# A two-layer decoder trunk on one core: weight sums of twelve pairs a layer built in DRAM by accumulating transfers, and the last down block as seven products

## Chip, core and metric

The kernel runs on one core of a Trainium2 chip. The metric is the device time of one execution in microseconds. The kernel before was timed three times: 1818.12, 1818.70 and 1818.74 us, with a median of 1818.7 us. A separate execution was profiled; all durations of single instructions come from it.

The engines are named as in the profile: PE multiplies matrices (PEld is its load of stationary operands), DVE, ACT and POOL work elementwise, SP issues most DMAs. POOL can issue DMAs as well, and only its DMAs can accumulate into their destination.

## The reference

The trunk has two layers on 512 tokens of width 1024, in float32. The part that matters here is the feed-forward half of a layer, with W1 of 1024 x 4096 and W2 of 4096 x 1024:

```python
def hybrid_layer(x, ...):
    ...
    x = x + rmsnorm(mix, post_mix_g)

    h2 = rmsnorm(x, pre_mlp_g)
    ff = jnp.square(jax.nn.relu(h2 @ w_ff1)) @ w_ff2
    return x + rmsnorm(ff, post_mlp_g)
```

Ahead of it in each layer come one wide projection, a gated delta rule, a banded attention with sinks, two up-projections and an output projection (`mix`). The change leaves their matrix products as they are.

## The kernel before

**Products.** Each float32 operand is split in two fp32r parts, a rounded one (`wh`, `P_h`) and the rest (`wl`, `P_l`), and each product is three matmuls: high x high, high x low, low x high. The split of a weight block `wr` of 128 x 1024 costs a cast on ACT (L384) and a subtraction on DVE (L385). `weights()` hands the blocks out in the order of `chunk_order` and prepares them four ahead (`LOOK = 4`, four buffers each of `wh` and `wl`); `wr` has six buffers, filled by DMAs that SP issues.

**Feed-forward.** The 4096 hidden units go in four blocks `s` of 1024, each as eight units `m` of 128. A block is first computed ("up", `ff1`) and then multiplied with its 1024 rows of W2 ("down"); `acc[t][n]` holds the sum over the blocks for token tile `t` (128 tokens) and column half `n`. A single unit is 24 matmuls of 512 columns (L400 to L402). A pair of units, written as a tuple in `SEQ`, is computed by seven products of half size instead of eight: 84 matmuls of 256 columns (L487 to L490). It needs two sums of the weight blocks, which DVE makes with four additions of 128 x 512 (L343). Before the change `SEQ` holds no pair in block 0, two in block 1, three in block 2 and four in block 3, nine in a layer.

**Down.** Blocks 0 to 2 take seven products too: P1 to P7, each 24 matmuls of 512 columns (`mm_c`, L475 to L479), with left factors from the hidden units (`lefts`, `make`) and right factors that are sums of W2 blocks (`seven`, additions at L304 and L309). The seven run in the order P1, P5, P6, P2, P7, P3, P4; P6 continues on a negated copy of P1's result (`py`), and P7 on a copy of P6's (`pw_`). Block 3 is an ordinary product: `mm_b4` for the first column half of all four token tiles (96 matmuls) and `last_tiles`, or a plain loop in the last layer, for the second half (96 matmuls), one token tile after the other, so that each tile's norm runs beside the next tile's matmuls.

**Norms.** `ff2_tail` calls `post_tiles`: a sum of squares on ACT (`meansq`, L520), a multiplication by the gain (L575), a power on POOL (`rstd`, L526), two multiply-adds with the residual (L578, L579) and, if another layer follows, the same once more for the next norm (L525, L535), ending in `xs`, which PE transposes (`norm_turn`, L546).

**Order.** Instructions are recorded in program order and a scheduler lays them out, one list for each engine; an engine runs its list in that order. `Order` pins some engines to program order for a stretch, and `tc.keep_in_program_order` does so for one instruction.

Of the kernel before, what the change touches and what calls it, by code (L numbers as in the profile page):

```python
# [15 lines left out]
ALU = mybir.AluOpType  # L16
# [28 lines left out]
SEQ = (FF_ORDER, (0, 1, (4, 5), (2, 3), 6, 7), ((0, 1), (4, 5), (2, 3), 6, 7), ((0, 1), (2, 3), (4, 5), (6, 7)))  # L45
# [12 lines left out]
def chunk_order(depth):  # L58
# [3 lines left out]
    for l in range(depth):  # L62
# [65 lines left out]
def hybrid_trunk(ctx, tc, x, positions, pre_mix_g, dn_conv_w, dn_a_log, dn_dt_bias, dn_norm_g,  # L128
# [162 lines left out]
    def seven(w, l, r0):  # L291
# [15 lines left out]
        def both(j):  # L307
# [10 lines left out]
                 lambda j: add(1, 0, j))  # L318
        return [(lambda f=f, j=j: f(j), 512) for f in makes for j in range(2)]


    def up_specs(l, s):
# [7 lines left out]
        def one(ms):  # L330
            b = {}

            def raw():
                b["0"], b["1"] = (unit(m) for m in ms)
                return b["0"]

            def of(n_):
                b[n_] = wp.tile([P, 1024], F32, name="wr", bufs=WR)
                x0, x1, x2, x3 = b["0"][:, :512], b["0"][:, 512:], b["1"][:, :512], b["1"][:, 512:]
                yb = b["a"][:, 512:]  # L340
                for o_, i0, i1 in (((b[n_][:, :512], x0, x2), (yb, b[n_][:, :512], x3)) if n_ == "a" else
                                   ((b[n_][:, 512:], x2, x3), (b[n_][:, :512], yb, x1))):
                    tt(out=o_, in0=i0, in1=i1, op=ALU.add)  # L343
                return b[n_]

            return raw, lambda: of("a"), lambda: of("b"), lambda: b["1"][:, 512:]
# [13 lines left out]
        return out + [(last, -1)] * bool(last)  # L360

# [104 lines left out]
    def mm_c(pss, left, onto=False, js=range(2)):  # L466

        for j in js:
            wh, wl = weights()
            hi, lo = left[j]  # L470
            for t in range(2):
# [87 lines left out]
    def post_tiles(tiles, a0g, ps1, q0, gb, xsrc, xdst, gb2=None, Tx=(T[5], T[6], T[7])):  # L559


        n = range(len(tiles))
        rows = [slice(t * P, (t + 1) * P) for t in tiles]
# [10 lines left out]
        for i, t in enumerate(tiles):  # L574
            tt(out=xo[i][:, 512:], in0=a[i], in1=gb[:, 512:], op=ALU.mult)  # L575
            r.append(rstd("pr", q0[t], q1[i]))
        for i, t in enumerate(tiles):
            stt(out=xo[i][:, :512], in0=a0g[t], scalar=r[i], in1=xt[i][0], op0=ALU.mult, op1=ALU.add)  # L578
            stt(out=xo[i][:, 512:], in0=xo[i][:, 512:], scalar=r[i], in1=xt[i][1], op0=ALU.mult,  # L579
                op1=ALU.add)  # L580
            xdst(t, xo[i])
# [23 lines left out]
    for l in range(depth):  # L605
# [437 lines left out]
        late, klate = (), []  # L1043
        for i in range(16):
            us = []
# [249 lines left out]
        for m in range(KT):  # L1295
# [5 lines left out]
            steps(2 if m < 6 else 40)  # L1301
            if m == 1:
                turn0()
# [66 lines left out]
        mm_b4(pss, mT)  # L1370
        m0, s0 = [], []
# [51 lines left out]
        def ff2_tail(tiles, pss):  # L1423
            a0 = [a[0] for a in acc]
            Tx = T[0], T[3], T[6]
            if l == depth - 1:
                post_tiles(tiles, a0, pss, s0, gb3, xd, give, None, Tx)
            else:
                xs_next.extend(post_tiles(tiles, a0, pss, s0, gb3, xd, keep, nxt[0], Tx))
# [35 lines left out]
        def ff1(done, rest=None):  # L1465
# [4 lines left out]
            for n, e in enumerate(SEQ[s]):  # L1470
                if not isinstance(e, tuple):
# [35 lines left out]
                mm_h(y, c2, 4, ops["n2"], False)  # L1507
# [5 lines left out]
                mm_h(z, c2, 0, ops["n1"], False)  # L1513
# [18 lines left out]
        for s in range(3):  # L1532
# [9 lines left out]
            def lefts(X, Y):  # L1542

                a11, a21, a12, a22 = X[:, 0:512], X[:, 512:1024], Y[:, 0:512], Y[:, 512:1024]
                make("P1", T[5], a11)
# [5 lines left out]
                make("P4", T[2], a22, -1.0)  # L1551
# [142 lines left out]
```

## Time and profile before

| what | value |
|---|---|
| median of three runs | 1818.7 us |
| profiled execution, device time | 1816.19 us |
| its span | 1814.5 us |
| granted TensorE clock, mean | 0.999 |
| ACT busy | 1007.5 us (56%) |
| POOL busy | 210.6 us (12%) |
| DMA | 278.60 MB, mean 154 GB/s |
| first layer, from the first down product to the next layer's first matmul | 625.8 to 909.7 us |

The profiled execution is 2.5 us, or 0.14%, under the median; 1.7 us of its time lie outside the span. In the profile, a timeline row gives the start, the duration, the engine and line, and in brackets how long the engine had stood idle and what ended that. Matmuls overlap, so their pace is read from the distance of their starts and not from the duration of one.

### The profile page before, as it was taken

Reading aid. Unit: us, or ns where it says so; the run is one execution under the profiler, and the core shown is the slowest. Engines: PE = TensorE matmul, PEld = TensorE weight load, DVE = VectorE, ACT = ScalarE, POOL = GpSimd, SP = SyncE. Lnnn points to the kernel's source line nnn. Section 1 sums busy time; section 2 is a strip of 40 time slices with the busy share of each in tenths; the row PEclk is TensorE's granted clock in tenths of the full one; section 3 lists DMA queues with packets and bytes.
Section 4 is the critical chain, followed back from the end, with each engine's and each line's share of the span. In section 5 each row is a group of like instructions: output and inputs, shape, how many; then the busy total and the mean of one; then the engine's idle time right before and its main releaser. Section 6 shows DMA issues by size and latency. Waiting matters only on the chain.

```text
span 1814.5 us, 28394 instructions
## 1 busy us (share of the span) xinstructions
PE 1794.6 (99%) x10252; PEld 1524.7 (84%) x10252; DVE 1375.1 (76%) x2590; ACT 1007.5 (56%) x2065; POOL 210.6 (12%) x386
## 2 busy tenths in 40 slices
PE   9999999999999999999999999999999999999998
PEld 8878878888788888989898887888877888889896
DVE  5499796887666878898556997968875669698973
ACT  6678742444434656566556877234443347566572
POOL 0322102221101000000013221022111010000000
PEclk9999999999999999999999999999999999999999
DMA  5633447655463254554445334585545533555551
GB/s 201 203 112 121 111 146 226 178 172 152 117 208 129 82 164 156 174 180 145 168 160 176 106 127 111 169 232 159 163 140 154 171 116 105 174 162 164 174 178 56
DMA packets 146431, 278.60 MB, mean 154 GB/s; under 512 B 33569, under 2 KB 66657, under 8 KB 146290
## 3 DMA queue, kind: packets, MB, share of 16 engines
q1 hardware_dynamic: 145778, 276.75, 49.2%
q8 instruction: 81, 1.33, 0.3%
q14 instruction: 60, 0.49, 0.1%
q0 software_dynamic: 512, 0.03, 0.0%
HBM read 239.38 MB, written 37.36 MB: 153 GB/s over the span
## 4 chain that ended last, share of the span: by engine, by line
PE 88%; DVE 4%; ACT 4%; DMA 2%; issue 1%; POOL 0%; SPq 0%; DVEq 0%; POOLq 0%; ACTq 0%
PE ps_b L459 3%; PE ps_b L461 3%; PE ps_b L463 3%; PE ps_f L400 2%; PE ps_f L401 2%; PE ps_f L402 2%; PE ps_us L400 2%; PE ps_ud L400 2%; PE ps_us L401 2%; PE ps_ud L401 2%; PE ps_ud L402 2%; PE ps_us L402 2%; PE ps_vp L400 2%; PE ps_vp L402 2%; PE ps_vp L401 1%; PE ps_qp L401 1%
## 5 line engine op out<-in xcount | busy, mean ns | idle before, releaser
L384 ACT CAST wh<-wr 128x1024 fp32r<-128x1024 f32 (+2 forms) x368 | 372.7, 1019 | 430.4 <-PE ps_us L401 60.2
L385 DVE TENSOR_TENSOR wl<-wr,wh 128x1024 fp32r<-128x1024 f32 (+2 forms) x368 | 434.9, 1189 | 183.8 <-ACT wh L384 180.2
L526 POOL TENSOR_TENSOR pr<-pq,pw 128x1 f32<-128x1 f32 x16 | 9.8, 615 | 790.1 <-DVE pq L525 790.1
L459 PE MATMUL ps_b<-wh,h_h 128*128 128x432 f32 (+1 forms) x192 | 71.1, 370 | 0.0
L461 PE MATMUL ps_b<-wl,h_h 128*128 128x432 f32 (+1 forms) x192 | 70.4, 367 | 0.0
L463 PE MATMUL ps_b<-wh,h_l 128*128 128x432 f32 (+1 forms) x192 | 70.3, 366 | 0.0
L400 PE MATMUL ps_f<-g_h,wh 128*128 128x512 f32 x160 | 62.4, 390 | 0.0
L401 PE MATMUL ps_f<-g_l,wh 128*128 128x512 f32 x160 | 62.4, 390 | 0.0
L402 PE MATMUL ps_f<-g_h,wl 128*128 128x512 f32 x160 | 62.2, 389 | 0.0
L401 PE MATMUL ps_qp<-h_l,wh 128*128 128x512 f32 x128 | 53.9, 421 | 0.0
L400 PE MATMUL ps_vp<-h_h,wh 128*128 128x512 f32 x128 | 53.7, 420 | 0.0
L402 PE MATMUL ps_vp<-h_h,wl 128*128 128x512 f32 x128 | 53.7, 419 | 0.0
L995 ACT ACTIVATE M<-M,nm 128x128 f32<-128x128 f32 x128 | 49.8, 391 | 5.9 <-DVE nm L990 5.8
L400 PE MATMUL ps_qp<-h_h,wh 128*128 128x512 f32 x128 | 51.8, 405 | 0.0
L343 DVE TENSOR_TENSOR wr<-wr 128x512 f32<-128x512 f32 x72 | 47.5, 685 | 5.5 <-DMA wr<-in_weights_dram 5.2
L400 PE MATMUL ps_kp<-h_h,wh 128*128 128x512 f32 x128 | 51.6, 403 | 0.0
L402 PE MATMUL ps_qp<-h_h,wl 128*128 128x512 f32 x128 | 51.4, 401 | 0.0
L401 PE MATMUL ps_vp<-h_l,wh 128*128 128x512 f32 x128 | 51.3, 401 | 0.0
L401 PE MATMUL ps_ga<-h_l,wh 128*128 128x512 f32 x128 | 51.0, 398 | 0.0
L400 PE MATMUL ps_gb<-h_h,wh 128*128 128x512 f32 x128 | 51.0, 398 | 0.0
L402 PE MATMUL ps_kp<-h_h,wl 128*128 128x512 f32 x128 | 50.9, 398 | 0.0
L402 PE MATMUL ps_ga<-h_h,wl 128*128 128x512 f32 x128 | 50.7, 396 | 0.0
(435 smaller groups left out, 5928.4 us busy)
## 6 DMA issues: line engine op xcount, KB each, us to landing
wr<-in_weights_dram SPq DMA_DIRECT2D x320, 512.0 KB, 3.6
wr<-in_weights_dram SPq DMA_DIRECT2D x24, 432.0 KB, 5.2
D<-dd SPq DMA_DIRECT2D x32, 256.0 KB, 2.7
xd<-xo SPq DMA_DIRECT2D x12, 512.0 KB, 3.0
xt<-xd SPq DMA_DIRECT2D x24, 256.0 KB, 4.5
D<-gd SPq DMA_DIRECT2D x16, 256.0 KB, 6.2
dd<-D SPq DMA_DIRECT2D x16, 256.0 KB, 5.2
kkd<-kk SPq DMA_DIRECT2D x16, 256.0 KB, 2.0
```

The source lines that it names most:

```text
L343: tt(out=o_, in0=i0, in1=i1, op=ALU.add)
L384: nc.scalar.copy(wh[:, :w], wr[:, :w])
L385: sub(out=wl[:, :w], in0=wr[:, :w], in1=wh[:, :w].bitcast(F32), op=ALU.subtract)
L400: mm(ps, lhsT=wh[:, k, :], rhs=hi, start=k == 0, stop=False)
L401: mm(ps, lhsT=wh[:, k, :], rhs=lo, start=False, stop=False)
L402: mm(ps, lhsT=wl[:, k, :], rhs=hi, start=False, stop=k == KT - 1)
L459: mm(pss[t], lhsT=hi[:, tsl], rhs=wh[:, r, :], start=k == 0 and not onto, stop=False, skip_group_check=onto)
L461: mm(pss[t], lhsT=hi[:, tsl], rhs=wl[:, r, :], start=False, stop=False, skip_group_check=onto)
L463: mm(pss[t], lhsT=lo[:, tsl], rhs=wh[:, r, :], start=False, stop=k == KT - 1, skip_group_check=onto)
L526: ptt(out=r, in0=q1, in1=mhalf[:, 0:1], op=ALU.pow)
L995: act(out=M[:, j * P:(j + 1) * P], in_=M[:, j * P:(j + 1) * P], func=AF.Exp, bias=nm[:, j:j + 1], accum_out=den[:, j:j + 1])
```

## The change

**Pairs.** Blocks 1, 2 and 3 now run as four pairs each, twelve in a layer. The weight sums of a pair are made in DRAM scratch: `prepare` copies the two units' blocks there with two SP DMAs of 512 KB, then POOL issues three accumulating DMAs of 512, 256 and 256 KB. Each of the fifteen calls of `next(ready)` in a layer starts one pair and moves up to three others on by one stage. `one` then loads the finished sums, two whole blocks and a half, in the place of DVE's additions.

**Down block 3.** It runs as seven products like the others, in the order P1, P5, P6, P2, P3, P7, P4. Before P2 and P3, DVE adds the accumulated `acc` of token tiles 0 and 1 onto the partial results in PSUM (`pa`, `pv`). After P3, tiles 0 and 1 are complete and `ff2_tail` runs for both; after P7, DVE puts `acc` of tiles 2 and 3 onto `pw_`, and P4 completes them. In the last layer P4 runs for tile 2 first and then for tile 3. P1's left factor is made earlier, and in the order of PSUM pools `pa` and `py` change places in blocks 1 to 3.

```diff
-SEQ = (FF_ORDER, (0, 1, (4, 5), (2, 3), 6, 7), ((0, 1), (4, 5), (2, 3), 6, 7), ((0, 1), (2, 3), (4, 5), (6, 7)))
+FF_PAIRS = ((0, 1), (4, 5), (2, 3), (6, 7))
+SEQ = (FF_ORDER, FF_PAIRS, FF_PAIRS, FF_PAIRS)
...
             out.append(("up", l, s))
-            if s < 3:
-                out.append(("seven", "w_ff2", l, s * 1024))
-                continue
-            for n in range(2):
-                for j in range(4):
-                    b_in("w_ff2", s * 1024 + j * 256, n * 512, 512)
+            out.append(("seven", "w_ff2", l, s * 1024))
...
+        if r0 == 3072:
+            makes = makes[:4] + (makes[5], makes[4], makes[6])
...
         def one(ms):
-            b = {}
-
-            def raw():
-                b["0"], b["1"] = (unit(m) for m in ms)
-                return b["0"]
-
-            def of(n_):
-                b[n_] = wp.tile([P, 1024], F32, name="wr", bufs=WR)
-                x0, x1, x2, x3 = b["0"][:, :512], b["0"][:, 512:], b["1"][:, :512], b["1"][:, 512:]
-                yb = b["a"][:, 512:]
-                for o_, i0, i1 in (((b[n_][:, :512], x0, x2), (yb, b[n_][:, :512], x3)) if n_ == "a" else
-                                   ((b[n_][:, 512:], x2, x3), (b[n_][:, :512], yb, x1))):
-                    tt(out=o_, in0=i0, in1=i1, op=ALU.add)
-                return b[n_]
-
-            return raw, lambda: of("a"), lambda: of("b"), lambda: b["1"][:, 512:]
+            d = sums[l, s, ms]
+
+            def of(c, w=1024):
+                wr = wp.tile([P, 1024], F32, name="wr", bufs=WR)
+                dma(wr[:, :w], d[:, c * 1024:c * 1024 + w])
+                return wr
+
+            def tail():
+                wr = wp.tile([P, 1024], F32, name="wr", bufs=WR)
+                dma(wr[:, :512], wpk[index["w_ff1", l, 0, (s * 8 + ms[1]) * P, 0], :, 512:])
+                return wr
+
+            return lambda: unit(ms[0]), lambda: of(0), lambda: of(1), tail
...
+    pairs = [(s_, e) for s_, seq in enumerate(SEQ) for e in seq if isinstance(e, tuple)]
+    sums = {(l, *p): dr.tile([P, 2048], F32, name=f"fs{l}{p[0]}{p[1][0]}")
+            for l in range(depth) for p in pairs}
+    def prepare(l):
+        here = tc.keep_in_program_order
+        def stages(s_, e):
+            i = index["w_ff1", l, 0, (s_ * 8 + e[0]) * P, 0]
+            assert index["w_ff1", l, 0, (s_ * 8 + e[1]) * P, 0] == i + 1
+            v = sums[l, s_, e][:, :].rearrange("p (h t c) -> p h t c", h=2, t=2)
+            for t in range(2):
+                here(dma(v[:, :, t, :], wpk[i + t].rearrange("p (h c) -> p h c", h=2)))
+            yield
+            here(pdma(v[:, :, 1, :], wpk[i:i + 2, :, 0:512].rearrange("t p c -> p t c"),
+                      accum_op=ALU.add))
+            yield
+            here(pdma(v[:, 0, 0, :], v[:, 1, 1, :], accum_op=ALU.add))
+            yield
+            here(pdma(v[:, 1, 0, :], v[:, 0, 0, :], accum_op=ALU.add))
+        todo = [stages(*p) for p in pairs]
+        for n in range(len(todo) + 3):
+            for g in todo[max(n - 3, 0):n + 1]:
+                next(g, None)
+            yield
...
+        ready = prepare(l)
         for i in range(16):
+            if i in (0, 2, 4, 6, 8, 11, 14):
+                next(ready)
...
-        for s in range(3):
+        for s in range(4):
...
+                if ms[-1] in (1, 3):
+                    make("P1", T[5], raw[0][:, 0:512])
...
             make_later("P3", T[1])
+            if s == 3:
+                break
...
-        ff1(done, pending)
-        pss = [b("ps_b4") for b in (PZ, PS, PS, PZ)]
-        for t in range(NT):
-            nc.scalar.copy(pss[t], acc[t][0])
-        mm_b4(pss, h3, onto=True)
-        for t in range(NT):
-            s0[t] = meansq(pss[t], "pq0")
-            tt(out=acc[t][0], in0=pss[t], in1=gb3[:, :512], op=ALU.mult)
-        ws = [weights() for _ in range(4)]
+        def early_half(t, n, src):
+            s0[t] = meansq(src, "pq0")
+            tt(out=acc[t][n], in0=src, in1=gb3[:, n * 512:(n + 1) * 512], op=ALU.mult)
+        for t in range(2):
+            tt(out=pa[t], in0=pa[t], in1=acc[t][0], op=ALU.add)
+            tt(out=pv[t], in0=pv[t], in1=acc[t][1], op=ALU.add)
         if l < depth - 1:
             nxt = pre_begin(l + 1)
             xs_next = []
+        mm_c(pa, left["P2"], True)
+        for t in range(2):
+            early_half(t, 0, pa[t])
+        mm_c(pv, left["P3"], True)
+        ff2_tail((0, 1), pv)
+        mm_c(pw_, left["P7"], True)
+        for t in range(2):
+            tt(out=acc[2 + t][1], in0=pw_[t], in1=acc[2 + t][1], op=ALU.add)
+            tt(out=pw_[t], in0=acc[2 + t][0], in1=pw_[t], op=ALU.subtract)
+        for t in range(2):
+            early_half(2 + t, 1, acc[2 + t][1])
+        if l < depth - 1:
             order = Order(nc.tensor)
             order.begin()
-            last_tiles(ws, h3, "ps_f2", ff2_tail, lambda t: norm_turn(xs_next[t], t, nxt[1]),
-                       [a[1] for a in acc])
+            for j in range(2):
+                mm_c(pw_, left["P4"], True, (j,))
+                norm_turn(xs_next[j], j, nxt[1])
+            ff2_tail((2, 3), pw_)
             hT = nxt
         else:
-            for t in range(NT):
-                ps = (PS if t % 2 else PZ)("ps_f2")
-                nc.scalar.copy(ps, acc[t][1])
-                mm_b(ps, ws, h3, t, onto=True)
-                ff2_tail((t,), [ps])
+            ws = [weights() for j in range(2)]
+            for t in range(2):
+                mm_c(pw_, left["P4"], True, ts_=(t,), ws=ws)
+                ff2_tail((2 + t,), pw_[t:])
```

**How the rows move.** The first place is DVE's list in the first layer's block 3. The names end in the program's buffer numbers: `ps_b4` are the four results of `mm_b4`, `h3_l` a split hidden unit, `ps_py`, `ps_pa` and `ps_pv` the partial results of P6, P1/P2 and P5/P3. Before, ahead of the first tile's norm:

```order
L501 TENSOR_TENSOR h3_l_9220<-raw_9051,h3_h_9219 128x512
L385 TENSOR_TENSOR wl_9264<-wr_9261,wh_9263 128x1024
L385 TENSOR_TENSOR wl_9294<-wr_9291,wh_9293 128x1024
L385 TENSOR_TENSOR wl_9324<-wr_9321,wh_9323 128x1024
L1653 TENSOR_TENSOR acc_6596<-ps_b4_9223,gb_8672 128x512
L1653 TENSOR_TENSOR acc_6598<-ps_b4_9224,gb_8672 128x512
```

And now, from P6 to P2:

```order
L409 TENSOR_TENSOR wl_9593<-wr_9590,wh_9592 128x1024
L1448 TENSOR_TENSOR acc_6665<-ps_py_9508,acc_6665 128x512
L1448 TENSOR_TENSOR acc_6667<-ps_py_9509,acc_6667 128x512
L525 TENSOR_TENSOR P3_l_9613<-S2_9206,P3_h_9612 128x512
L1683 TENSOR_TENSOR ps_pa_9468<-ps_pa_9468,acc_6664 128x512
L525 TENSOR_TENSOR P3_l_9617<-S2_9451,P3_h_9616 128x512
L1684 TENSOR_TENSOR ps_pv_9520<-ps_pv_9520,acc_6665 128x512
L1683 TENSOR_TENSOR ps_pa_9469<-ps_pa_9469,acc_6666 128x512
```

The additions onto `ps_pa` stand behind the two that read P6's result `ps_py`. On PE, the same place now reads:

```order
L503 MATMUL ps_py_9509<-wh_9525,P6_l_9459 128x512
L499 MATMUL ps_pa_9468<-wh_9543,P2_h_9512 128x512
L501 MATMUL ps_pa_9468<-wl_9544,P2_h_9512 128x512
L503 MATMUL ps_pa_9468<-wh_9543,P2_l_9513 128x512
L499 MATMUL ps_pa_9468<-wh_9543,P2_h_9512 128x512
L501 MATMUL ps_pa_9468<-wl_9544,P2_h_9512 128x512
L503 MATMUL ps_pa_9468<-wh_9543,P2_l_9513 128x512
L499 MATMUL ps_pa_9469<-wh_9543,P2_h_9512 128x512
```

P2, which writes `ps_pa`, follows P6 directly there; six matmuls go onto `ps_pa_9468` before the first onto `ps_pa_9469`.

The second place is DVE's list at the end of the first layer, around the norms of tiles 0 and 1. Before, where `xo` and `xs` belong to one tile at a time:

```order
L575 TENSOR_TENSOR xo_9430<-ps_f2_9397,gb_8672 128x512
L525 SCALAR_TENSOR_TENSOR pq1_9432<-pq1_9432,pq0_9352 128x1
L578 SCALAR_TENSOR_TENSOR xo_9430<-acc_6596,pr_9435,xt_9426 128x512
L579 SCALAR_TENSOR_TENSOR xo_9430<-xo_9430,pr_9435,xt_9427 128x512
L525 SCALAR_TENSOR_TENSOR nq1_9445<-nq1_9445,nq0_9442 128x1
L535 SCALAR_TENSOR_TENSOR xs_9450<-xo_9430,nr_9447,gb_9391 128x512
L535 SCALAR_TENSOR_TENSOR xs_9452<-xo_9430,nr_9447,gb_9391 128x512
L575 TENSOR_TENSOR xo_9483<-ps_f2_9398,gb_8672 128x512
```

And now, from the last multiply-add of tile 1 on, where `ps_pw` is the result of P7 that P4 goes on with:

```order
L604 SCALAR_TENSOR_TENSOR xo_9728<-xo_9728,pr_9740,xt_9722 128x512
L549 SCALAR_TENSOR_TENSOR nq1_9753<-nq1_9753,nq0_9750 128x1
L409 TENSOR_TENSOR wl_9779<-wr_9382,wh_9778 128x1024
L559 SCALAR_TENSOR_TENSOR xs_9764<-xo_9727,nr_9761,gb_9626 128x512
L559 SCALAR_TENSOR_TENSOR xs_9766<-xo_9727,nr_9761,gb_9626 128x512
L549 SCALAR_TENSOR_TENSOR nq1_9759<-nq1_9759,nq0_9756 128x1
L409 TENSOR_TENSOR wl_9797<-wr_9794,wh_9796 128x864
L559 SCALAR_TENSOR_TENSOR xs_9771<-xo_9728,nr_9768,gb_9626 128x512
L559 SCALAR_TENSOR_TENSOR xs_9773<-xo_9728,nr_9768,gb_9626 128x512
L1695 TENSOR_TENSOR acc_6669<-ps_pw_9569,acc_6669 128x512
L1696 TENSOR_TENSOR ps_pw_9569<-acc_6668,ps_pw_9569 128x512
```

The two additions on `ps_pw_9569`, which P4 waits for, stand behind the whole norm chain of both tiles. In the second layer no next norm follows, and between the last multiply-add and the additions stands one `wl` row alone.

The third place is POOL's list beside the attention of the first layer, where `pc` is a masked probability tile that PE multiplies next, `irk` a power of the key norms, and `fs` a pair's scratch. Now:

```order
L1042 AFFINE_SELECT pc_1515<-pf_l_1510 128x512
L378 DMA fs010_112<-fs010_112 128x512
L376 DMA fs014_113<-fs014_113 128x512
L373 DMA fs012_114<-in_weights_dram 256x1x512
L854 TENSOR_TENSOR irk_1576<-ssk_1570,pw_93 128x4
L1042 AFFINE_SELECT pc_1652<-pf_h_1648 128x512
```

Before, the same rows stand there without the three DMAs.

More of the change, by code (lines that the diff above doesn't have):

```diff
@@ L1370, in hybrid_trunk @@
         mm_b4(pss, mT)
+        next(ready)
         m0, s0 = [], []
@@ L1584, in hybrid_trunk @@
                     done((m,), ps)
+                    if s == 0 and i in (1, 5):
+                        next(ready)
                     if s == 0 and i in (1, 3, 5):
```

46 lines of the change are left out of this document (23 added, 23 removed).

## The prediction

> **What bounds the kernel now.** I read the page's busy shares first, then PE's own list of waits, then the pace of its matmuls, and last who works beside it in a down block.
>
> ```profile
> span 1814.5 us, 28394 instructions
> PE 1794.6 (99%) x10252; PEld 1524.7 (84%) x10252; DVE 1375.1 (76%) x2590; ACT 1007.5 (56%) x2065; POOL 210.6 (12%) x386
> PE 88%; DVE 4%; ACT 4%; DMA 2%; issue 1%; POOL 0%; SPq 0%; DVEq 0%; POOLq 0%; ACTq 0%
> ```
>
> PE is busy for 99% of the span and holds 88% of the chain that ended last. So the time is the number of matmuls at their pace, plus whatever makes PE wait. Its longest waits of before, from the view of waits on PE alone:
>
> ```profile
> PE ps_pt L1007 <- ACT M L1001: 3.9, 6, 0.8
> PE ps_row L602 <- DMA row<-in_pre_mix_g_dram: 2.3, 1, 2.3
> ```
>
> The first lies in the attention, the second at the start; no line of the feed-forward is worth a microsecond. The pace comes from the timeline of PE: the first and last of 97 matmuls of 256 columns in a row, and of 24 of 512 columns.
>
> ```profile
> 759.83 0.28 PE L490 MATMUL ps_q<-n_h,wl 128*128 128x256 f32 x1
> ...
> 771.35 0.28 PE L490 MATMUL ps_z<-n_h,wl 128*128 128x256 f32 x1
> ```
>
> ```profile
> 606.57 0.39 PE L402 MATMUL ps_f<-g_h,wl 128*128 128x512 f32 x1
> ...
> 611.78 0.39 PE L401 MATMUL ps_f<-g_l,wh 128*128 128x512 f32 x1
> ```
>
> The distance of starts is 11.52/96 = 0.120 us for 256 columns and 5.21/23 = 0.2265 us for 512. The 0.28 and 0.39 us in the rows overlap and would be wrong as a price: by them a pair would cost more than two single units.
>
> Who has room beside PE? One down block of before and the up block behind it, DVE alone:
>
> ```profile
> 785.63:826.00 40.37, 38.88 (x47) 1.00 0.49 156
> ```
>
> DVE is busy for 38.88 of 40.37 us. In a down block PE is the bound by a hair, and DVE, which makes weight splits, weight sums and left factors, is the engine that any new dependency meets.
>
> **The change part by part.**
>
> **Matmuls.** Three pairs a layer replace six single units: 6 x 24 = 144 matmuls of 512 columns go and 3 x 84 = 252 of 256 come. The last down block goes from 192 to 168, and one filler matmul (L1603) is added. Over two layers that is 2 x (-144 - 24 + 1) = -334 matmuls of 512 and +504 of 256: -334 x 0.2265 + 504 x 0.120 = -75.7 + 60.5 = **-15.2 us**. A pair saves only 10.88 - 10.08 = 0.8 us, the down block 5.4.
>
> **DVE's pair sums.** They go:
>
> ```profile
> L343 DVE TENSOR_TENSOR wr<-wr 128x512 f32<-128x512 f32 x72 | 47.5, 685 | 5.5 <-DMA wr<-in_weights_dram 5.2
> ```
>
> The 47.5 us lie beside PE's matmuls in up blocks, where PE does not wait, so I count them at nothing.
>
> **From P6 to P2, twice.** Here a wait is added: P2 must find `acc` already added onto `pa`. P6 and its neighbours already run in the blocks before, so their rows price it. DVE, ACT and PE there (the PE rows are the first of the block, that is of P1, and the first after P6; the last fence has DVE's first row of the block):
>
> ```profile
> 796.82 2.36 DVE L385 TENSOR_TENSOR wl<-wr,wh 128x1024 fp32r<-128x1024 f32 x2
> 799.10 0.68 DVE L1417 TENSOR_TENSOR acc<-ps_pv,acc 128x512 f32<-128x512 f32 x1
> ...
> 802.57 1.28 DVE L1417 TENSOR_TENSOR acc<-ps_py,acc 128x512 f32<-128x512 f32 x2
> 803.77 0.68 DVE L501 TENSOR_TENSOR P_l<-S,P_h 128x512 fp32r<-128x512 f32 x1
> ```
>
> ```profile
> 801.03 0.57 ACT L1606 COPY ps_pw<-ps_py 128x512 f32<-128x512 f32 x1 [0.96 <-PE ps_py L479]
> 802.39 0.57 ACT L1606 COPY ps_pw<-ps_py 128x512 f32<-128x512 f32 x1 [0.79 <-PE ps_py L479]
> ```
>
> ```profile
> 785.63 0.39 PE L475 MATMUL ps_pa<-wh,P_h 128*128 128x512 f32 x1
> ...
> 802.19 0.39 PE L475 MATMUL ps_pa<-wh,P_h 128*128 128x512 f32 x1
> ```
>
> ```profile
> 787.85 0.69 DVE L1547 TENSOR_TENSOR S<-raw 128x512 f32<-128x512 f32 x1
> ```
>
> DVE paces a 128 x 512 row at 0.60 us (802.57 to 803.77 holds two) and a 128 x 1024 row at 1.14 (796.82 to 799.10 holds two). P6's halves can be read 1.16 us before and 0.20 us after its end. In the order of the change, DVE has 13 short and 7 long rows between the first `S` and the first `acc<-ps_py`: 13 x 0.60 + 7 x 1.14 = 15.8 us. `S` starts 2.2 us after P1 (787.85, with P1 at 785.63), and P6 ends 3 x 5.44 + 0.23 = 16.55 us after P1's start, so that `acc<-ps_py` starts 1.45 us after the end of P6. Then come two `acc`, one `P3_l` and the first `ps_pa`: 4 x 0.60, and P2 starts at 3.85. Three short rows more, and the second `ps_pa` is ready at 5.65, where P2 wanted it at 1.36. PE loses 4.3 us a layer, **+8.6 us**. Bounds: with an idle DVE the rows can begin at 0.20 and the loss is 2.45 us; with the weight splits late by 0.7 us it is 5.0.
>
> **From P7 to P4, twice.** Count from the moment the second `ps_pa` is ready. PE ends P3 9.5 us later (P2 and P3 are 48 matmuls, less the first six: 42 x 0.2265) and P7 at 15.0. DVE first has 3 short and 8 long rows, 10.9 us, and stands about 1.15 us behind a weight sum whose cast ACT must make first. The norms of tiles 0 and 1 start at 12.05, 2.5 us after the end of P3. Rows of the same chain at the layer's end before:
>
> ```profile
> 910.72 0.69 DVE L575 TENSOR_TENSOR xo<-ps_f,gb 128x512 f32<-128x512 f32 x1 [0.55 <-ACT jk L520]
> 911.33 0.15 DVE L525 SCALAR_TENSOR_TENSOR pq<-pq,pq 128x1 f32<-128x1 f32 x1
> ...
> 912.06 0.75 DVE L579 SCALAR_TENSOR_TENSOR xo<-xo,pr,xt 128x512 f32<-128x512 f32 x1
> 912.72 0.75 DVE L578 SCALAR_TENSOR_TENSOR xo<-acc,pr,xt 128x512 f32<-128x512 f32 x1
> 913.38 0.75 DVE L579 SCALAR_TENSOR_TENSOR xo<-xo,pr,xt 128x512 f32<-128x512 f32 x1
> 914.04 0.15 DVE L525 SCALAR_TENSOR_TENSOR nq<-nq,nq 128x1 f32<-128x1 f32 x1
> 914.11 1.05 DVE L385 TENSOR_TENSOR wl<-wr,wh 128x864 fp32r<-128x864 f32 x1
> ...
> 917.81 1.42 DVE L535 SCALAR_TENSOR_TENSOR xs<-xo,nr,gb 128x512 f32<-128x512 f32 x2 [0.72 <-POOL nr L526]
> ```
>
> Two `xo` and two sums take 1.45 us and four multiply-adds at 0.66 take 2.65; with what POOL leaves open they end 6.8 us after P3. In the second layer one split (1.14) and two additions (1.2) follow: P4 may start at 9.15, P7 ended at 5.44, a loss of 3.7 us. In the first layer the split, two times two `xs` (1.33 each), a split of 864 columns (1.0) and POOL's round trips stand ahead of the additions, which end at 13.05: 7.6 us. Together **+11.3 us**. Bounds: had DVE no backlog, the norms would start 2.95 us sooner, with 1.2 and 5.0 us lost, POOL's turns taking some of it back; another microsecond late makes 4.7 and 8.6. Queued behind the additions are the splits for the next layer's first block, which are not needed for another 5 us.
>
> **The clock.** After its last matmul, starting at 1807.04, PE stands idle:
>
> ```profile
> 1807.50:1810.50 3.00, 0.00 (x0) 0.00 (x0) 1.51 (x4) 0.69 (x2) 0.54 (x1) 1.00 0.00 0
> 1811.00:1814.50 3.50, 0.00 (x0) 0.00 (x0) 0.16 (x1) 0.00 (x0) 0.00 (x0) 0.50 0.40 150
> ```
>
> The 1.00 and the 0.50, third from the end of a row, are the granted clock: it falls to half within 3.7 us. The first layer's idle of 7.6 us is longer than that, so P4 begins at half clock. If its first twelve matmuls ran so, they would cost 2.7 us more; at nothing if the clock came back at once. No row tells; I take the middle, **+1.4 us**. The Trainium skill, "TensorE: Matmul & The Clock Gate", part 1, has a clock that halves after about 3.4 us of idleness and returns after about 3.4 us of work; the trace agrees with the fall, and by that figure the cost would be some 1.7 us, an estimate by that page.
>
> **The end.** P4 gives tile 3 only 12 matmuls after tile 2, and the norm of tile 2 still holds DVE.
>
> ```profile
> 1808.27 0.69 DVE L575 TENSOR_TENSOR xo<-ps_f,gb 128x512 f32<-128x512 f32 x1 [2.55 <-ACT jk L520]
> ```
>
> Before, tile 3's `xo` started about 1.0 us after PE's end; now 1.3: **+0.3 us**, between 0 and 0.6.
>
> **Transfers.** Twelve pairs add 25 MB of copies and accumulations a layer, and pairs and down block load some 14 MB more: 78 MB on 278.60 in all. They lie beside PE; a weight block is asked for four blocks ahead, and a load takes 3.6 us:
>
> ```profile
> wr<-in_weights_dram SPq DMA_DIRECT2D x320, 512.0 KB, 3.6
> ```
>
> Four blocks are 10.9 us in a down block. I count nothing. Without that cover, one late load would cost its delay.
>
> **The sum** is -15.2 + 8.6 + 11.3 + 1.4 + 0.3 = +6.4 us on the profiled 1816.19, that is 1822.6. The runs' median is 2.5 us higher; I put the same step on it: **1825 us**.
>
> **The rivals.** *A, the forecast*: DVE's backlog makes PE wait in both places, 1825 us.
>
> *B, the chains alone*: DVE is not behind when P6 ends, since its pair sums are gone. The waits are the lower bounds: -15.2 + 4.9 + 6.2 = -4.1, 1814.6 us. For it: DVE enters the block with less work. Against: 20 rows still stand between `S` and `acc<-ps_py`.
>
> *C, nothing waits*: the additions are ready in time and all 15.2 us stay, 1803.5 us. P6's result is needed by rows that stand ahead of `ps_pa` on DVE, which speaks against it.
>
> *D, slower still, by POOL*: its accumulating DMAs stand between the rows that feed the attention.
>
> ```profile
> L1216 POOL DMA_DIRECT2D fd<-ff x16: 590/620/757, 348.9 to 1393.3; - x16
> ...
> DMA to landing us min/median/max: 1.7/2.4/4.5
> ```
>
> ```profile
> 145.74 0.64 POOL L1017 TENSOR_SCALAR_AFFINE_SELECT pc<-pf_l 128x512 fp32r<-128x512 f32 x1 [0.68 <-DVE es L992]
> 151.56 0.64 POOL L1017 TENSOR_SCALAR_AFFINE_SELECT pc<-pf_h 128x512 fp32r<-128x512 f32 x1 [5.18 <-ACT pf_h L500]
> ```
>
> Three DMAs at 0.62 us fit in the 5.2 us of idle time ahead of `pc`; from 1.7 us each they delay it. If each held POOL for the 2.4 us of its landing, two such places a layer would lose 2 us each, +8.4 in all: 1833.5 us on top of A. Sixteen small issues of before never took over 0.76 us. The Trainium skill, "DMA: Bandwidth & Descriptors", SWDGE vs HWDGE vs iDMA, says that POOL writes descriptors into SBUF and can be locked out by DVE's two-port mode; that would be such a hold, and the sixteen rows do not show it.
>
> **How the numbers follow.** A 0.55, B 0.20, C 0.07, D 0.15, and 0.03 for what I do not see. The range leaves out C, half of D and some tails: 1812 to 1834 us. What a measurement can tell from no change is 0.2%, 3.6 us: faster is below 1815.1, C and half of B, 0.17; same reaches to 1822.3, the other half of B and A's low tail, 0.22; slower has the rest, 0.61.
>
> **What would show it.** The profile after should have PE's waits list headed by `ps_pa` and `ps_pw` behind DVE's additions (L1683, L1696), about 4 us at P6's end in both layers, 7 to 8 us at P4 in the first and under 4 in the second, and no such rows in blocks 1 and 2. The clock should dip at the first layer's end. If these rows are small, DVE was not behind and B or C holds; if the attention's waits grow past 3.9 us, D. The forecast is wrong if a short row on DVE does not cost 0.60 us there, or if the weight sums arrive late.

## The result, and the profile after

The changed kernel takes **1848.07 us** (median of four runs, 1846.96 to 1853.36), the kernel before in the same session 1818.72 us: a ratio of **1.0166, 95% interval 1.0146 to 1.0186**. It is slower, by 29 us where the prediction had 6, and the time lies 14 us above the predicted range. The profiled execution took 1848.6 us against 1816.19, 32.4 us more.

From the page of the changed kernel, the span, the engines' busy time and the chain that ended last by engine:

```profile
span 1846.9 us, 29182 instructions
PE 1794.6 (97%) x10422; PEld 1529.7 (83%) x10422; DVE 1412.4 (76%) x2622; ACT 1040.2 (56%) x2117; POOL 278.8 (15%) x458
PE 78%; DVE 10%; DMA 4%; ACT 4%; issue 2%; POOL 1%; SPq 0%; DVEq 0%; POOLq 0%; ACTq 0%
```

PE's busy time is the same to the tenth, although its matmuls should take 15.2 us less, and its part of the chain has fallen from 88% to 78%. So PE waits, and some matmuls run slower. PE's own longest waits (total, how often, longest):

```profile
PE ps_pa L499 <- DVE ps_pa L1683: 10.1, 2, 5.0
PE ps_ud L425 <- DVE yT_l L525: 10.0, 2, 5.5
PE ps_pw L499 <- DVE ps_pw L1696: 9.3, 2, 7.0
PE ps_pt L1032 <- ACT M L1026: 3.9, 6, 0.8
```

The first and the third are the two waits of the prediction. The second, in the up-projection behind the delta rule, is not in it at all. Each comes once a layer. What follows each of them is seen in windows of PE (start and end, length, PE's busy time with the number of its matmuls in brackets, granted clock, DMA share, GB/s), here before, in and behind the first wait for `ps_pa`, with two short windows left out:

```profile
889.60:890.40 0.80, 0.59 (x3) 1.00 0.83 164
...
890.80:893.20 2.40, 0.00 (x0) 1.00 0.79 213
...
893.60:894.00 0.40, 0.00 (x0) 0.82 0.61 246
894.00:895.20 1.20, 0.00 (x0) 0.50 0.85 208
895.20:900.40 5.20, 5.18 (x12) 0.50 0.28 75
900.40:900.80 0.40, 0.40 (x2) 0.65 0.71 276
900.80:902.00 1.20, 1.20 (x7) 1.00 1.11 372
```

The clock falls to half after 3.7 us without a matmul and stays there for 6.8 us. Twelve matmuls start in 5.2 us, one in 0.43 us in the place of 0.2265. It is so behind all six waits, the one of 2.3 us in the second layer too: 58 matmuls at half pace, which with the steps into and out of it cost 12.7 us in all (distances of starts, less 0.2265 each).

The second wait, in the first layer, can be followed back. Here are POOL's list at the end of the delta rule, SP's load of `fb`, and the DVE rows that need it:

```profile
497.11 0.61 POOL L1244 DMA_DIRECT2D fd<-ff  x1 [0.30 <-POOL ff L1243]
497.72 0.94 POOL L378 DMA_DIRECT2D fs<-fs  x1
498.30 1.21 POOL L376 DMA_DIRECT2D fs<-fs  x1
498.85 1.74 POOL L373 DMA_DIRECT2D fs<-in_weights_dram  x1
```

```profile
503.07 0.32 SPq L1247 DMA_DIRECT2D fb<-fd  x1
```

```profile
512.11 0.69 DVE L1248 TENSOR_TENSOR yf<-yf,fb 128x512 f32<-128x512 f32 x1 [13.63 <-DMA fb<-fd]
513.01 1.29 DVE L525 TENSOR_TENSOR yT_l<-yf,yT_h 128x512 fp32r<-128x512 f32 x2 [0.20 <-DVE yf L1248]
```

`fd`, 2 KB, leaves POOL at 497.7 and SP can load it back at 503.07, 5.4 us later; `fb` reaches DVE 9.0 us after that. The kernel before has at the same places, on SP and DVE:

```profile
497.85 0.32 SPq L1219 DMA_DIRECT2D fb<-fd  x1
```

```profile
502.75 0.69 DVE L1220 TENSOR_TENSOR yf<-yf,fb 128x512 f32<-128x512 f32 x1 [7.43 <-DMA fb<-fd]
```

There `fd` left POOL at 495.1, so the two legs took 2.8 and 4.9 us. Between `fd` and `fb` the program issues nothing new but three accumulating DMAs, 1 MB together, which POOL issues the moment `fd` is out. The share of the 16 DMA engines in both legs, first before and then after:

```profile
495.10:497.90 2.80, 2.80 (x14) 1.00 0.64 240
497.90:502.70 4.80, 4.80 (x22) 1.00 0.75 124
```

```profile
497.70:503.10 5.40, 5.40 (x25) 1.00 1.01 174
503.10:512.10 9.00, 6.18 (x28) 0.97 1.04 224
```

In the changed kernel the engines are full (a share of 1.0) and yet move less, 174 and 224 GB/s, than in another full window (372 GB/s above).

### The profile page after: what moved, and what is told of

Read it like the earlier page. It is cut to its first block, busy times and chain, and to the rows that moved or that the text cites. A ratio compares the mean times of both kernels' runs of the same rounds, so it can differ in the third digit from the quotient of the medians.

```text
span 1846.9 us, 29182 instructions
## 1 busy us (share of the span) xinstructions
PE 1794.6 (97%) x10422; PEld 1529.7 (83%) x10422; DVE 1412.4 (76%) x2622; ACT 1040.2 (56%) x2117; POOL 278.8 (15%) x458
## 2 busy tenths in 40 slices
DMA packets 182148, 356.25 MB, mean 193 GB/s; under 512 B 36514, under 2 KB 69602, under 8 KB 182003
## 3 DMA queue, kind: packets, MB, share of 16 engines
q1 hardware_dynamic: 168050, 329.19, 56.8%
q0 software_dynamic: 13952, 25.20, 9.1%
## 4 chain that ended last, share of the span: by engine, by line
PE 78%; DVE 10%; DMA 4%; ACT 4%; issue 2%; POOL 1%; SPq 0%; DVEq 0%; POOLq 0%; ACTq 0%
PE ps_b L483 2%; PE ps_b L485 2%; PE ps_b L487 2%; DVE wl L409 2%; PE ps_vp L424 2%; PE ps_us L424 2%; PE ps_vp L426 2%; PE ps_us L425 2%; PE ps_us L426 2%; PE ps_vp L425 2%; PE ps_qp L425 1%; PE ps_qp L424 1%; PE ps_qp L426 1%; DMA fb<-fd 1%; PE ps_zp L425 1%
## 5 line engine op out<-in xcount | busy, mean ns | idle before, releaser
L425 PE MATMUL ps_ud<-yT_l,wh 128*128 128x512 f32 x128 | 52.4, 410 | 10.0 <-DVE yT_l L525 10.0
L499 PE MATMUL ps_pa<-wh,P_h 128*128 128x512 f32 x128 | 51.9, 405 | 10.1 <-DVE ps_pa L1683 10.1
L300 DVE TENSOR_TENSOR wr<-wr 128x1024 f32<-128x1024 f32 x48 | 57.8, 1218 | 1.9 <-DMA wr<-in_weights_dram 1.7
L511 PE MATMUL ps_z<-n_h,wh 128*128 128x256 f32 x192 | 55.0, 286 | 0.0
L514 PE MATMUL ps_a<-g_h,wl 128*128 128x256 f32 x192 | 54.3, 283 | 0.0
L513 PE MATMUL ps_a<-g_l,wh 128*128 128x256 f32 x192 | 54.3, 283 | 0.0
L514 PE MATMUL ps_z<-n_h,wl 128*128 128x256 f32 x192 | 54.3, 283 | 0.0
L511 PE MATMUL ps_a<-g_h,wh 128*128 128x256 f32 x192 | 54.3, 283 | 0.0
L513 PE MATMUL ps_z<-n_l,wh 128*128 128x256 f32 x192 | 54.3, 283 | 0.0
L426 PE MATMUL ps_ud<-yT_h,wl 128*128 128x512 f32 x128 | 51.6, 403 | 0.0
## 6 DMA issues: line engine op xcount, KB each, us to landing
fs<-in_weights_dram POOLq DMA_DIRECT2D x24, 512.0 KB, 10.2
```

What stands on the lines that cost most here:

```text
L300: tt(out=held[j], in0=held[j], in1=part(i, k, j), op=ALU.add)
L425: mm(ps, lhsT=wh[:, k, :], rhs=lo, start=False, stop=False)
L426: mm(ps, lhsT=wl[:, k, :], rhs=hi, start=False, stop=k == KT - 1)
L499: mm(pss[t], lhsT=hi[:, c], rhs=wh[:, r, :], start=first, stop=False, skip_group_check=onto)
L511: mm(ps, lhsT=wh[:, k0 + k, :], rhs=hi, start=start and k == 0, stop=False, skip_group_check=True)
L513: mm(ps, lhsT=wh[:, k0 + k, :], rhs=lo, start=False, stop=False, skip_group_check=True)
```

## The experiments

The runs come from several chips. All ratios are to the kernel before on the same chip, with a 95% interval, so it is the ratios that compare across rows. The waits are totals over both layers, in us, from one profiled execution of each run; "none" is less than 0.5 us.

| run | what it is | median us | ratio | PE's waits: `ps_pa`, `yT_l`, `ps_pw` |
|---|---|---|---|---|
| changed | | 1848.07 | 1.0166 (1.0146 to 1.0186) | 10.1, 10.0, 9.3 |
| e1 | pairs only | 1828.43 | 1.0071 (1.0054 to 1.0088) | none, 6.2, none |
| e2 | last down block only | 1836.85 | 1.0112 (1.0096 to 1.0127) | 10.3, none, 9.2 |
| e3 | one stage of the preparation later | 1835.57 | 1.0103 (1.0088 to 1.0118) | 10.1, none, 9.1 |
| e4 | the stage's three DMAs with few bytes | 1834.5 | 1.0101 (1.0086 to 1.0116) | 10.1, 0.5, 9.2 |
| e5 | `pa` added early | 1841.87 | 1.0137 (1.0123 to 1.0151) | 0.7, 7.8, 13.2 |
| e6 | `ps_pw` ahead of next norm | 1848.31 | 1.017 (1.0156 to 1.0184) | 10.1, 7.7, 10.2 |
| e7 | e3, e5 and e6 together | 1831.28 | 1.0076 (1.0062 to 1.0089) | 0.7, none, 14.4 |
| e8 | e2 with e5 and e6 | 1831.95 | 1.0081 (1.0068 to 1.0095) | 1.0, none, 14.4 |
| e9 | e7, sums by POOL | 1845.84 | 1.015 (1.0136 to 1.0164) | none, none, 12.1 |
| e10 | e1 with e3 | 1818.4 | 1.0003 (0.9994 to 1.0011) | none, 0.8, none |
| e11 | e8, sums by POOL | 1846.77 | 1.0156 (1.0141 to 1.0172) | none, none, 13.7 |
| e12 | e7, W2 sums of block 3 left out | 1812.25 | 0.9976 (0.9965 to 0.9987) | none, none, 3.5 |
| e13 | e7, sums from DRAM | 1823.12 | 1.0035 (1.0023 to 1.0047) | none, none, 3.5 |
| e14 | e8, sums from DRAM | 1827.64 | 1.0054 (1.0041 to 1.0068) | none, none, 3.5 |
| e15 | e13, spread out | **1812.79** | **0.9978 (0.9969 to 0.9987)** | none, none, 3.5 |

**The two halves apart.** e1 keeps the last down block of before, e2 the nine pairs and DVE's sums of before:

```diff
-            out.append(("seven", "w_ff2", l, s * 1024))
+            if s < 3:
+                out.append(("seven", "w_ff2", l, s * 1024))
+                continue
...
-SEQ = (FF_ORDER, FF_PAIRS, FF_PAIRS, FF_PAIRS)
+SEQ = (FF_ORDER, (0, 1, (4, 5), (2, 3), 6, 7), ((0, 1), (4, 5), (2, 3), 6, 7), FF_PAIRS)
```

> The twelve pairs with their sums in DRAM alone; the last down block is the ordinary product of before. Theory 1 (the accumulating DMAs that POOL issues right behind the last fd fill the DMA engines, so that fd and fb land late and PE waits for yT_l): -4.8 us of matmuls, +15 in the up-projection of both layers (10 of waiting, 5 of half clock), some +4 in small waits: 1831 to 1836 us, with PE's wait for yT_l at 9 to 11 us. Rival (the wait comes from the last down block's extra loads or a general shortage of bandwidth over the whole kernel): no wait for yT_l, 1813 to 1817 us.

> The seven products in the last down block alone; pairs as before, with their sums by DVE (only the order of the pairs in block 3 is that of the changed kernel). Theory: -10.4 us of matmuls, +10.4 of waiting from P6 to P2, +9.7 from P7 to P4, +8 of half clock behind these four waits: 1834 to 1840 us, and no wait for yT_l. Rival (DVE is late at P6 because of what the twelve pairs changed, not because of the block itself): waits under 3 us each, 1815 to 1825 us.

e2 came as expected: the block alone has both of its waits, so they do not come from what the pairs changed elsewhere. e1 has the wait for `yT_l` and nothing of the other two, but 6.2 us of it in the place of 9 to 11, and 1828 us in the place of 1831 to 1836: the place is right, the size was taken from one profile and varies. The profiled execution of e1 was also the shortest of its four (1822.61 us, the longest 1831.43).

**Whose bytes.** e3 moves the stage (its three accumulating DMAs and two copies) past the norms of the output projection; e4 leaves it where it is and thins its three accumulating DMAs to 32 of 512 columns, which leaves the weight sums of three pairs a layer incomplete:

```diff
         mm_b4(pss, mT)
-        next(ready)
...
+        next(ready)
         acc = [[US("acc") for n in range(2)] for t in range(NT)]
```

```diff
+            w1, w2, w3 = (32 if n_ == k else 512 for k in (9 - 1, 9 - 2, 9 - 3))
-            here(pdma(v[:, :, 1, :], wpk[i:i + 2, :, 0:512].rearrange("t p c -> p t c"),
+            here(pdma(v[:, :, 1, :w1], wpk[i:i + 2, :, 0:w1].rearrange("t p c -> p t c"),
```

> The changed kernel with one stage of the preparation (two SP copies and three accumulating DMAs, in each layer) moved from behind the last fd of the delta rule to behind the norms of the output projection. Theory 1: the waits for yT_l and their half clock go, -13 to -16 us against the changed kernel: 1832 to 1835 us. Rival (fb is late because of the loads that SP issues there, or because of lost slack): within 3 us of the changed kernel, 1845 to 1851 us.

> The changed kernel with the same three accumulating DMAs behind the last fd, in the same place and number and with the same rows, but 32 columns each in the place of 512 (so the weight sums of three pairs a layer are left incomplete). Theory 1 in the form of a fight for bytes: fd and fb land as before, the waits for yT_l fall under 2 us in all: 1832 to 1837 us. Rival (it is the issue or the queue of POOL, or the number of rows, and not the bytes): the waits stay near 10 us: 1845 to 1850 us.

Both take the wait away. In e4 POOL issues the same three DMAs with the same durations (0.94, 1.21, 1.74 us) at the same place, and yet `fb` starts 3.9 us after `fd` has left and DVE reads it 4.0 us later (500.41 and 504.36). So it is the bytes on the DMA engines, not POOL's time or its list, that made `fd` and `fb` late. The gain, 11 to 12 us by the ratios, is a little less than the 13 to 16 expected of e3.

**The order on DVE.** e5 records the additions onto `pa` ahead of P6; e6 records P7 and the additions on `ps_pw` between the multiply-adds and the next norm:

```diff
+            if s == 3:
+                for t in range(2):
+                    tt(out=pa[t], in0=pa[t], in1=acc[t][0], op=ALU.add)
             mm_c(py, left["P6"], True)
```

```diff
+        mid()
         xs = []
         if gb2 is not None:
...
-        ff2_tail((0, 1), pv)
-        mm_c(pw_, left["P7"], True)
+        ff2_tail((0, 1), pv, seventh_product)
```

> The changed kernel with the additions of acc onto pa recorded ahead of P6, so that DVE no longer has them behind the rows that read P6's result. Theory 2a (the order on DVE alone makes P2 wait): both waits for ps_pa and the half clock behind them go, -13 to -15 us: 1833 to 1835 us. Theory 2b (DVE has more work in this block than PE, so a wait that goes comes back at the next place where PE needs DVE): the waits for ps_pa go, those for ps_pw grow from 7.0 and 2.3 us to about 12 and 6, net -4 to -8 us: 1840 to 1844 us.

> The changed kernel with P7 and the additions on ps_pw recorded between the multiply-adds and the next norm's part of the chain for tiles 0 and 1. Theory 3 (P4 waits because the whole chain stands ahead): the first layer's wait of 7.0 us falls to 1 to 2 us, the norm's result is then 1 to 2 us late for its transposition, the second layer keeps its 2.3 us: -4 to -8 us, 1840 to 1844 us. Rival (the transposition then waits as long as P4 did): within 2 us of the changed kernel.

> The changed kernel with the stage of preparation moved (as in the third run), the additions onto pa early and those on ps_pw ahead of the next norm. Theory 2b: the gains of the stage (12 to 14 us) and of the other two (10 to 14 us together) add up, 1820 to 1826 us, still not faster than before. Theory 2a: all 48 us of new waits but some 8 go, 1806 to 1810 us.

> The seven products alone (pairs as before) with both additions moved. Theory 2b: like the run with all three, without the 4.8 us that the pairs save and without their small waits: 1818 to 1828 us. Theory 2a: 1808 to 1812 us.

e5 falls to theory 2b: all but 0.7 us of the wait for `ps_pa` is gone, and 4 us of it are back at `ps_pw`. (The wait for `yT_l`, which the edit does not touch, happens to be 2.2 us shorter in this profile.) e6 gains nothing, its rival's time, but not by the rival's way: the transposition does not wait, `ps_pw` still does (6.5 us at its longest). P7's own calls of `weights()`, now recorded there, brought a weight sum and two splits for P4 with them, ahead of the additions. In e7 and e8 the waits for `ps_pw` total 14.4 us, more than e5's 13.2, and the times came out 5 and 4 us above the ranges of theory 2b. DVE in e7 between the additions on `ps_pv` and those on `ps_pw` (length, DVE busy with its rows, clock, DMA share, GB/s):

```profile
888.20:906.90 18.70, 17.18 (x22) 0.96 0.77 263
```

DVE has 17.2 us of work there, and PE works for 10.9 us from P3's beginning to P7's end (48 matmuls). With this much work in the stretch, the two moves only passed the wait on. The norm rows that still stand in it could be put later too; that was not tried.

**Less work for DVE.** The sums of right factors in this block (L300, L305) are eight rows of 1.14 us a layer. e9 and e11 give them to POOL, e12 leaves them out:

```diff
+        on = ptt if r0 == 3072 else tt
...
-            tt(out=held[j], in0=held[j], in1=part(i, k, j), op=ALU.add)
+            on(out=held[j], in0=held[j], in1=part(i, k, j), op=ALU.add)
```

```diff
+            b = part(i, k, j)
+            if r0 == 3072:
+                held[j] = b
```

> The run with all three edits, and the eight sums of right factors in the last down block made by POOL in the place of DVE (L300, L305; DVE takes 1.14 us for each, four of them between the additions on ps_pv and those on ps_pw). Theory 2b (DVE's work in this block is the bound): the waits for ps_pw fall from 7.7 and 6.7 us by about 4.6 us each, and some of the half clock goes: 10 to 14 us less than with the three edits, 1817 to 1821 us. Rival (it is the order and the chain, not the amount of work on DVE; or POOL, at about 2.5 us a sum, is late itself): within 3 us of the run with three edits, 1828 to 1834 us, with PE or DVE waiting for POOL.

> The seven products alone (pairs as before) with both additions moved and the block's sums on POOL. Theory 2b: 10 to 14 us less than the run of the seven products with the two moves alone: 1818 to 1822 us. Rival: within 3 us of it.

> The twelve pairs alone (the last down block as before) with the stage of preparation moved. By the count of matmuls -4.8 us against before, +2 to +4 for the small waits that DMA loads and POOL add: 1814 to 1816 us where the kernel before has 1816.5, the same within the measurement. If the pairs cost more than the delta rule's end (a shortage of bandwidth elsewhere), 1820 us or more.

> The run with all three edits, and in the last down block the eight sums of right factors left out: every block is loaded, but P5, P6, P7 and P4 multiply with a single weight block in the place of the sum. DVE loses 8 x 1.14 = 9.1 us of work a layer, and unlike in the run with the sums on POOL nothing takes its place. Theory 2b (the amount of DVE's work between P5 and P4 is the bound): the waits for ps_pw fall from 7.7 and 6.7 us by 4 to 5 us each and part of the half clock goes: 1817 to 1823 us. Theory 2c (P4 waits for the chain of norm rows, casts and POOL's turns, whatever else DVE does): the waits fall by less than 2 us each, 1827 to 1831 us.

e9 and e11 are slower than e7 and e8, by 13 to 15 us. Both have a new wait, in P5, for a left factor that DVE makes (`ps_pv` behind `P_l`, 6.3 and 6.2 us). POOL and DVE in e9, in the first layer:

```profile
866.58 2.51 POOL L301 TENSOR_TENSOR wr<-wr 128x1024 f32<-128x1024 f32 x1 [1.16 <-DVE wl L410]
870.25 2.42 POOL L301 TENSOR_TENSOR wr<-wr 128x1024 f32<-128x1024 f32 x1 [1.16 <-DVE wl L410]
```

```profile
866.76 3.42 DVE L410 TENSOR_TENSOR wl<-wr,wh 128x1024 fp32r<-128x1024 f32 x1
870.10 0.41 DVE L1557 TENSOR_TENSOR raw<-ps_y,raw 128x256 f32<-128x256 f32 x1
870.43 3.32 DVE L410 TENSOR_TENSOR wl<-wr,wh 128x1024 fp32r<-128x1024 f32 x1
...
877.05 1.21 DVE L410 TENSOR_TENSOR wl<-wr,wh 128x1024 fp32r<-128x1024 f32 x1
```

Each time the DVE row ends 1.1 us after POOL's, as if it had begun when POOL ended: 3.3 to 3.4 us for a row that takes 1.2 without POOL. So a sum on POOL, with such a DVE row beside it, takes 2.1 to 2.2 us from DVE, where its own takes 1.14. The Trainium skill, "SBUF — State Buffer", Who interferes with whom, says that a DVE instruction with two inputs in SBUF contends with a GpSimd instruction that reads SBUF, and that the shared ports are an exclusive lock; these rows agree, 2.2 us lost beside a POOL row of 2.5. So e9 made more work for DVE, not less, and says nothing against theory 2b.

e12, where nothing takes the place of the 9.1 us, decides for it against theory 2c: 18 us less than e7 by the ratios, the waits for `ps_pw` 3.5 us in all, and a mean granted clock of 0.999 in the place of 0.994. That is more than the 8 to 14 expected. Four of the eight rows, 4.6 us, lie in the stretch above, and the wait fell by 5.5 us a layer; so the amount of DVE's work explains most of it, and the rest may be what waits behind a sum (in e7 DVE stands idle for 1.1 us there until ACT has cast one). The half clock behind the waits went with them.

e10 tells what the twelve pairs are worth: 4.8 us less matmul time, and no change in the time (1.0003), 2 us more than expected. The rest goes into waits that are each at most 1.3 us long and one of 1.8 us in the attention; which transfer makes which was not tried.

**A complete version.** e13 builds the eight sums in DRAM as the change does for the pairs, e14 does so with the pairs of before (`put` is a copy by SP, `plus` an accumulating DMA by POOL, `w(i, k, j)` a block of W2):

```diff
+        def four(j):
+            put("P7", j, w(0, 1, j))
+            put("P5", j, w(0, 0, j))
+            yield
+            put("P6", j, w(0, 0, j))
+            put("P4", j, w(1, 0, j))
+            plus("P7", j, w(1, 1, j))
+            plus("P5", j, w(0, 1, j))
+            yield
+            plus("P6", j, rights[l, "P7", j])
+            yield
+            plus("P4", j, rights[l, "P6", j])
```

> The run with all three edits, and the eight sums of right factors of the last down block built complete in DRAM during blocks 1 and 2 (16 more copies and 16 more accumulating DMAs of 512 KB over two layers), so that DVE makes none of them. Theory 2b: as in the run without the sums, waits for ps_pw of 1 to 2 us each, 1811 to 1816 us, faster than or the same as before. If the added 17 MB of transfers delay weight blocks in blocks 1 to 3: new waits for wh or wl there, 1818 to 1825 us.

> The same last down block with its eight sums from DRAM, but the pairs as before (nine a layer, sums by DVE, none in DRAM). By the count of matmuls 4.8 us more than with twelve pairs; if the pairs' transfers and POOL's part in them give these back, as the pairs alone suggest (1.0003 of before), the same as the run with twelve pairs within 2 us: 1810 to 1816 us.

> The run with the eight sums from DRAM, with its copies and accumulating DMAs issued one at a time, beside the pairs and products of blocks 1 and 2, in the place of two copies and up to three accumulations at once. If the transfers cost by standing together: the waits for wh in block 1 and the half clock behind them (about 6 us a layer) go, 1811 to 1815 us, faster than before by 0.1 to 0.4%. If they cost by their number: waits for wh or wl elsewhere in blocks 1 and 2, 1820 us or more.

e13's down block is as good as e12's (the same 3.5 us at `ps_pw`), but PE now waits for weight blocks (`wh`) in block 1, where SP and POOL issue the new transfers:

```profile
PE ps_pv L546 <- ACT wh L455: 6.0, 2, 3.0
PE ps_pt L1080 <- ACT M L1074: 4.0, 6, 0.8
PE ps_pw L546 <- DVE ps_pw L1754: 3.5, 2, 2.2
```

e14 is 4.5 us above e13, where 2 us at most were expected, and e13 itself came in the slower of its two ranges. Its list has waits of 3.3 us for `wh` and of 2.1 and 1.3 us in the pairs, for `wl`, where DVE must make their sums as well; so it doesn't tell the price of the pairs' transfers cleanly, and that stays open. e15 issues the same copies one at a time, beside the pairs of blocks 1 and 2:

```diff
             for n, e in enumerate(SEQ[s]):
...
+                if s in (1, 2):
+                    next(more)
```

PE's waits in e15:

```profile
PE ps_pt L1073 <- ACT M L1067: 3.9, 6, 0.8
PE ps_pw L539 <- DVE ps_pw L1749: 3.5, 2, 2.2
PE ps_row L668 <- POOL T L221: 2.5, 1, 2.5
PE ps_s L1043 <- DVE M L1051: 2.1, 2, 1.8
```

The wait for `wh` in block 1 is gone, as expected if the transfers cost by standing together, and at **1812.79 us the kernel is faster than both others**, if by little: 0.9978 (0.9969 to 0.9987) of the one before. Of the 15.2 us of matmuls that the change saves, about 4 us now remain.

## Why the prediction was wrong

The account, on the profiled executions (us; forecast, then what the trace has):

| step | forecast | measured |
|---|---|---|
| matmuls | -15.2 | -15.2 (by count and pace) |
| P6 to P2 | +8.6 | +10.1 |
| P7 to P4 | +11.3 | +9.3 |
| the clock | +1.4 | +12.7 |
| transfers (wait for `yT_l`) | 0 | +10.0 |
| the end | +0.3 | about 0 |
| what is left | 0 | +5.5 |
| sum | +6.4 | +32.4 |

- **Matmuls**: right. 170 more instructions, -334 and +504.
- **From P6 to P2**: the mechanism was right, the size short by 0.75 us a layer. The term that failed is where `S` starts: it was taken at 2.2 us behind P1, as in block 3 of before; P1 starts at 873.44 and three DVE rows of the changed kernel read

```profile
874.55 2.35 DVE L300 TENSOR_TENSOR wr<-wr 128x1024 f32<-128x1024 f32 x2
876.82 0.68 DVE L1580 TENSOR_TENSOR S<-raw 128x512 f32<-128x512 f32 x1
...
892.58 1.28 DVE L1448 TENSOR_TENSOR acc<-ps_py,acc 128x512 f32<-128x512 f32 x2
```

  that is 3.4 us, since two weight sums now stand ahead of it. The 15.8 us from there to `acc<-ps_py` are exact. Of the 4.3 us forecast, 0.44 were a second wait, six matmuls later; it did not come, because those six ran at half clock, and so 1.2 us more in front became 0.75 in all.
- **From P7 to P4**: right in place and cause, 7.0 us in the first layer (7.6 forecast) and 2.3 in the second (3.7). Together the two places cost 19.4 us against 19.9 forecast, by two errors that cancel. The prediction counted DVE's backlog, but not that DVE has more work here than PE, so that a wait removed at one place comes back at the next: theory 2b is the runs', not the prediction's.
- **The clock**: the step that failed most. The prediction had it fall once, behind the wait of 7.6 us, and cost 1.4 us (there it cost 1.6); it passed over its own two waits of 4.3 us, though they too are longer than the 3.7 us that it had read at the kernel's end. The clock fell behind all six waits, and cost 1.6 to 2.8 us at each; even the 3.7 us were no lower bound.
- **Transfers**: "I count nothing" was the other failure. The 78 MB are right (356.25 MB against 278.60), and the cover of four blocks did hold for the weight loads. But the added transfers also meet others, and two small ones, `fd` and `fb`, have PE behind them with no slack. The prediction quoted the row of `fd<-ff`, for rival D, and looked at POOL's time for issuing; the number that mattered stood below it, its landing, and who waits for that was not asked.
- **Rivals**: B and C are out, since all waits came. D was the nearest in time (1833.5 us; three holds of 2.4 us less 5.2 us of idle time, at four places, are 8.1 us on top of A and not 8.4) and named POOL's DMAs, but not the cause: e4 shows bytes and not POOL's time, and the attention's wait for ACT is 3.9 us as before.
- **What is left**: 5.5 us, which is what the other terms leave over; e10 gives back about as much in small waits. 1.8 us of it is a longer wait in the attention, for `ps_s`, behind a DVE row shown below; the rest stays open.

The signs that the prediction named came: `ps_pa` and `ps_pw` are among the three longest waits, and the clock dips at the first layer's end. It had no sign for the third name, `yT_l`, nor for a clock that falls elsewhere.

## What to carry to other kernels

When an engine has more work in a stage than the one that waits for it, moving its rows may only move the wait, as here, where taking work from it removed one: count both engines' work over the stretch between two places where they meet, before pricing a reorder. Extra DMA bytes "beside" other work were not free here where a short transfer with an engine behind it lay in the same microseconds, so look for the small round trips through DRAM first; and here bulk transfers cost less when they were issued one at a time. And a wait of some microseconds on PE is to be priced with the half clock behind it, here 1.6 to 2.8 us each.

## What the hardware showed that was not expected

- The granted clock does not need a long idle stretch. In e3, PE stood idle for 1.9 us in the attention, went on, and was then put to half clock for some 3 us (windows of PE as above; the first covers the next two and the microsecond ahead of them):

```profile
157.20:160.60 3.40, 1.51 (x8) 1.00 1.08 270
158.20:160.20 2.00, 0.13 (x1) 1.00 1.09 264
160.20:160.60 0.40, 0.38 (x3) 1.00 1.05 234
...
161.00:163.60 2.60, 2.60 (x10) 0.50 0.75 231
...
164.40:166.00 1.60, 1.60 (x8) 1.00 0.10 23
```

  In the changed kernel the same wait, as long, brought no half clock. The Trainium skill, "TensorE: Matmul & The Clock Gate", part 1, has a free-running window of about 3.4 us and a clock that halves after an idle one. The lengths of half clock agree, 3.4 us here and 6.8 us above; but the 3.4 us that end where the clock falls were busy for 1.51 us here, so that less than an idle window was enough, and the measurement decides.
- A DVE row of 128 x 128 took over 2 us in the attention, beside rows of POOL. Two such rows together, in the changed kernel and before:

```profile
156.04 2.33 DVE L525 TENSOR_TENSOR vp<-kv,vp 128x128 fp32r<-128x128 f32 x2 [0.86 <-ACT vp L524]
```

```profile
155.50 0.78 DVE L501 TENSOR_TENSOR vp<-kv,vp 128x128 fp32r<-128x128 f32 x2
```

  It looks like the lock of e9, but POOL's rows stand beside it before, too, and in e1, where the same two rows take 0.59 us; so standing side by side is not enough for it, and the cause stays open.
- Accumulating DMAs use the engines more than their bytes say: 25.20 MB on POOL's queue took 9.1% of the 16 engines' span, 329.19 MB on the other queue 56.8%, so a megabyte cost about twice as much.

```profile
q1 hardware_dynamic: 168050, 329.19, 56.8%
q0 software_dynamic: 13952, 25.20, 9.1%
```
